# Latent attention by head with a table rope, and modulation by array quarters, in a two-layer diffusion trunk

## The chip, the cores and the metric

The kernel runs on one core of a Trainium2 chip. The metric is the device time of one execution in microseconds; three runs of the kernel before took 1910.07, 1912.01 and 1912.65 us. Engines are named PE (TensorE, with PEld for its weight loads), DVE (VectorE), ACT (ScalarE), POOL (GpSimd) and SP (SyncE, which here only issues DMAs).

## The reference

Two layers work on 512 latent tokens and 256 context tokens of 1024 features, all in fp32. A layer computes a modulated RMSNorm, one input projection whose columns feed four mixers, an output projection, and a gated feed-forward block. The second layer makes no context output. What the change touches is the modulation and mixer D, multi-head latent attention (MLA):

```python
def mla_heads(p, q_norm, w_uq, kv_norm, w_ukv, cos, sin, use_rope):
    cq, ckv, k_rot = jnp.split(p, [MLA_Q_RANK, MLA_Q_RANK + MLA_KV_RANK], axis=-1)     # 192, 128, 32
    q = (rmsnorm(cq, q_norm) @ w_uq).reshape(b_sz, t_len, MLA_HEADS, MLA_NOPE + MLA_ROPE)   # 4 x (64 + 32)
    kv = (rmsnorm(ckv, kv_norm) @ w_ukv).reshape(b_sz, t_len, MLA_HEADS, MLA_NOPE + MLA_V_DIM)
    ...
    if use_rope:                                 # latent tokens only
        q_rot = apply_axial_rope(q_rot, cos, sin)
        k_rot = apply_axial_rope(k_rot, cos, sin)    # one rotary key for all four heads
```

Latent queries see all 768 keys, context queries (first layer only) the 256 context keys. The modulation is silu(c) times a matrix of 1024 x 6144 per layer, for the two vectors c and c_ctx; it gives six sections (shift, scale and gate of both halves) of 1024 features.

## The kernel before, in words

Activations stand feature by token: a tile is 128 features (partitions) by 768 tokens. Every product of fp32 operands is made of three matmuls of a rounded type (fp32r): each operand is split in a high part (ACT casts) and a low part (DVE subtracts in `split`, L136 to L138; POOL subtracts in `psplit`, L140 to L142), and high·high, low·high and high·low are summed in PSUM. All matmuls pass the helper `mm`, so they stand at line L134 and are told apart by their tiles. PSUM has two pools: `b2`, two tiles of two banks (scores `pss`, projections over all tokens), and `b1`, four tiles of one bank (all the rest: `psm`, `psq`, `psk`, `psv`, transposed probabilities `pspt`, values `psy`, output projection `pso`). SBUF tiles come from rotating pools `s3` (768 columns) and `w4` (1024 columns).

The program is written as Python generators; `run` interleaves several of them by weights (each `yield` ends a step), and a scheduler then fixes the order of each engine's queue ahead of time, by estimated times. The stage in question is L1248:

```python
        run((chain(scan(), late()), 1.0), (chain(some_mods(NS), mla_prologue(), attention(mla_halves)), WM))
```

The scan (mixer B, six chunks; tiles `pscr`, `pstt`, `psg`, `psyo`, `psyb`) runs beside, first, eight modulation chunks, then the MLA prologue, then the MLA attention. `late` splits the outputs of the mixers A, B and C for the output projection.

*Modulation* (`mod_chunks`, L196). A chunk makes 512 of the 6144 features. The vectors stand as 32 columns (two of them used) of a stationary operand, so a matmul fills 32 columns of the array; the four quarters of the array work on four k tiles at once, and the four partial sums stand in four groups of 32 PSUM rows. ACT copies the 128 x 512 result (`mrow`, L208), four fp32 products with the constant `sel` (two columns) add up the quarters and turn features to partitions, DVE adds the bias.

*MLA prologue* (`mla_prologue`, L1113). Values `vd` for the four heads; a query projection of all four heads' rotary rows (four times 32 rows) with rope by `rope` (L496: DVE shuffle and cosine product, POOL sine product, DVE add, into `qr`); then per pair of heads `get_pair`: query and key projections, and per head operands `dqh`, `dql`, `dkh`, `dkl` with 64 rows of the head, 32 rotary rows copied in from `qr` and `kr` (L1170, L1171, `psplit`), and 32 padded rows by POOL (L1154).

*The rotary key* `kr` is made far earlier, in the input projection, by the same `rope` on 32 rows (`q_then`, L842).

*Attention* (`attention`, L585) has a unit for each head and 128 queries: `scores` (scores in `pss`, row maximum on DVE L524, exponential on ACT L531, scaling on POOL L538), three units later `turn` (transposes `pspt`, split), then `values` (`psy`, L582 and L583). `AHEAD` = 10 units ahead of a unit's scores its operands are prepared. There are 20 units in the first layer and 16 in the second, where only latent tokens ask.

After the stage the output projection reads the split outputs (`pso`, `out_tile` L1258); its stream `x` is loaded by SP just ahead of it.

Of the kernel before, what the change touches and what calls it, by code (L numbers as in the profile page):

```python
# [34 lines left out]
AHEAD = 10  # L35
NA, NC, NS = 0, 0, 12
# [7 lines left out]
NP1 = 8  # L44
# [21 lines left out]
for _n, _w in PARTS:  # L66
# [4 lines left out]
CONSTS = [("ident", 128), ("ones", 128), ("sel", 2), ("fnw", 8), ("cosA", 512), ("sinA", 512), ("cosM", 512),  # L71
          ("sinM", 512), ("uf", 128), ("ub", 128), ("bones", 128)]
# [16 lines left out]
def trunk(ctx: ExitStack, tc: tile.TileContext, a, out):  # L89
# [106 lines left out]
    def mod_chunks(l, chs):  # L196
        for ch in chs:
# [16 lines left out]
            yield  # L214

# [266 lines left out]
    def mixers(l, norm, halfway, mods):  # L482
# [102 lines left out]
        def attention(halves):  # L585
# [5 lines left out]
            for i in range(n + LOOK + 1):  # L591
                for j in range(i, min(n, i + AHEAD + 1)):
# [225 lines left out]
        def norm_split(srcs, n, segs, res):  # L818
# [13 lines left out]
            for t, r, w in srcs:  # L832
                hi, lo = s3("chi", F32R), s3("clo", F32R)
# [8 lines left out]
        def q_then():  # L842
            mqn = tiny("mqn", 2)
            dve.tensor_scalar(mqn, par_at(l, "mqn", 0, 2), DS, None, op0=ALU.mult)
            kr.append(s3("kr"))
            rr = slice(64, 96)
            rope(kr[0], dq[1], C("cosM"), C("sinM"), SWAP8, rr)
            act.copy(kr[0][rr, CT], dq[1][rr, CT])
# [7 lines left out]
        d_items = [in_tile(T_DQ, qsegs, d_post(dq, qsegs, 128)), in_tile(T_DX, both, d_post(dq, both, 96, q_then), 96),  # L856
# [256 lines left out]
        def mla_prologue():  # L1113
            wq = [w4("wq", (2, 512)) for _ in range(2)]
            for i, (r, nm) in enumerate(((128, "wuqa"), (64, "wuqb"))):
                wr = w4("raw", (1024,), F32)
                nc.sync.dma_start(wr[:r, :384], a[nm][l])
                split(wq[0][:r, i, :384], wq[1][:r, i, :384], wr[:r, :384])
# [5 lines left out]
            (ckh, ckl), cqs = ckv[0], d_low  # L1124
            vd = [s3("vd", F32R, (6, 128)) for _ in range(4)]
            for j in range(6):
                ps = b1("psv")
                sl = slice(128 * j, 128 * j + 128)
                for jj, (hh, wi) in enumerate(((ckh, 0), (ckl, 0), (ckh, 1))):
                    mm(ps[:, 0:256], hh[:, sl], wk[:, wi, 256:512], jj == 0, jj == 2)  # L1130
                for hd in range(4):
                    split(vd[hd][:, j, 0:64], vd[hd][:, j, 64:128], ps[:, 64 * hd:64 * hd + 64])
                yield

            def up_q(t):
                ps = acc("psq", qsegs)
                for i, r in ((0, 128), (1, 64)):
                    for jj, (wi, lo) in enumerate(((0, 0), (0, 1), (1, 0))):
                        for s, p in zip(qsegs, ps):
                            mm(p, wq[wi][:r, i, 128 * t:128 * t + 128], cqs[i][lo][:r, SEG[s]], i == 0 and jj == 0,  # L1140
                               i == 1 and jj == 2)
                return ps

            ps = up_q(2)
            qr, qrw = s3("qr"), s3("qrw", F32, (SEQ,))
            act.copy(qrw, ps[0])
            rope(qr, qrw, C("cosM"), C("sinM"), SWAP8)
            if wc:
                act.copy(qr[:, CT], ps[1])
            yield  # L1150
            halves = mla_halves

            def pad_rows(t, w):
                pool.tensor_copy(t[96:128, :w].rearrange("p (a b) -> p a b", b=64),  # L1154
                                 ident[96:128, 0:64].unsqueeze(1).to_broadcast([32, w // 64, 64]))

            for pr in range(2):
                def get_pair(pr=pr):
                    qps = up_q(pr)
                    r = []  # L1160
                    for hh in range(2):
                        hd = 2 * pr + hh
                        rh = slice(64 * hh, 64 * hh + 64)
                        qh_, ql_ = s3("dqh", F32R), s3("dql", F32R)
                        for t in (qh_, ql_):
                            pad_rows(t, QW)
                        for s, p in zip(qsegs, qps):
                            split(qh_[0:64, SEG[s]], ql_[0:64, SEG[s]], p[rh])
                        q4 = qr[32 * hd:32 * hd + 32, :QW]
                        act.copy(qh_[64:96, :QW], q4)  # L1170
                        dve.tensor_tensor(ql_[64:96, :QW], q4, qh_[64:96, :QW].bitcast(F32), op=ALU.subtract)  # L1171
                        r.append([qh_, ql_])
                    kps = acc("psk", both)
                    for jj, (wi, hh) in enumerate(((0, ckh), (0, ckl), (1, ckh))):
                        for s, p in zip(both, kps):
                            mm(p, wk[:, wi, 128 * pr:128 * pr + 128], hh[:, SEG[s]], jj == 0, jj == 2)
                    for hh in range(2):
                        rh = slice(64 * hh, 64 * hh + 64)
                        kh_, kl_ = s3("dkh", F32R), s3("dkl", F32R)
                        for t in (kh_, kl_):  # L1180
                            pad_rows(t, TOK)
                        for s, p in zip(both, kps):
                            split(kh_[0:64, SEG[s]], kl_[0:64, SEG[s]], p[rh])
                        psplit(kh_[64:96], kl_[64:96], kr[0][64:96])
                        r[hh] += [kh_, kl_]
                    y_d.append(s3("yf"))
                    return r, y_d[-1]

                get_pair = once(get_pair)
                for hh in range(2):  # L1190
                    hd = 2 * pr + hh

                    def sc_mm(ps, q0, segs, get_pair=get_pair, hh=hh):
                        qh_, ql_, kh_, kl_ = get_pair()[0][hh]
                        qs = slice(q0, q0 + 128)
                        for jj, (q_, k_) in enumerate(((qh_, kh_), (ql_, kh_), (qh_, kl_))):
                            for o, sl in segs:
                                mm(ps[:, o:o + sl.stop - sl.start], q_[:, qs], k_[:, sl], jj == 0, jj == 2)

                    def yf(get_pair=get_pair):  # L1200
                        return get_pair()[1]

                    def vhl(hd=hd):
                        return vd[hd]

                    def no_sink():
                        return None

                    for hb in range(2):
                        def score(ps, qi, hb=hb, sc_mm=sc_mm):  # L1210
                            sc_mm(ps, 256 * hb + 128 * qi, ((0, LAT), (512, CT)))
                            return TOK, 0
# [381 lines left out]
```

## Time and profile before

| | |
|---|---|
| median of three runs | 1912.01 us (1910.07 to 1912.65) |
| the profiled execution | 1910.93 us, span 1909.1 us |
| PE busy | 1813.2 us (95%), 11552 matmuls |
| DVE / ACT / POOL busy | 1071.2 (56%) / 788.9 (41%) / 537.7 us (28%) |
| mean granted clock of PE | 0.975 |
| stage of layer 0, scan start to first `pso` | 320.65 to 472.42 us |
| first MLA scores, layer 0 / layer 1 | 406.81 / 1423.55 us |
| stage of layer 1 | 1345.61 to 1476.93 us |

The page puts the engines' slices over time, the chain of waits, and groups of instructions side by side. Busy shares are means over stages with different limits, so this stage is cut in windows: modulation with scan, prologue, attention. In the rows below "xN" counts instructions; a fp32 matmul that is not split stands as two. The bracket at a row's end is the time its engine waited ahead of it, and what released it. The granted clock has two levels, 1.2 and 2.4 GHz; PEclk is the mean over a stretch as a share of the upper one.

### The profile page before, as it was taken

How to read it: one execution, taken by the hardware profiler on the slowest of the kernel's cores; microseconds unless marked ns; L12 is line 12 of the kernel's file. 1: busy time of each engine (PE TensorE's matmuls, PEld its weight loads, DVE VectorE, ACT ScalarE, POOL GpSimd, SP SyncE). 2: the span in 40 equal slices, each digit the busy share in tenths (PEclk: the TensorE clock that was granted, in tenths of full speed). 3: DMA queues.
4: the chain of work that ended last, by engine and by line, in shares of the span. 5: the costliest groups of instructions: out<-in, count | busy, mean ns of one | idle time of the engine just before them, and what ended most of it. 6: DMA issues, size and time to landing. Idle time of an engine off the chain costs nothing. (4 is left out here: it accounts for less than half of the span.)

```text
span 1909.1 us, 29269 instructions
## 1 busy us (share of the span) xinstructions
PE 1813.2 (95%) x11552; PEld 1573.8 (82%) x11552; DVE 1071.2 (56%) x2058; ACT 788.9 (41%) x1506; POOL 537.7 (28%) x565
## 2 busy tenths in 40 slices
PE   6989999978999999999999999999988999999997
PEld 3978898757888888888888888989767888888886
DVE  4564674467355444554553474677367565555545
ACT  3475564457243222222222354655447352323222
POOL 0353421544155143122230054440344210000001
PEclk9999899989999999999999999999979999999999
DMA  8101016303212222222221210103703322323221
GB/s 314 42 12 45 24 56 247 119 1 133 78 56 80 87 89 78 78 81 75 88 68 56 95 50 12 56 23 123 288 1 109 100 79 88 111 83 117 78 89 55
DMA packets 50568, 165.19 MB, mean 87 GB/s; under 512 B 5632, under 2 KB 9600, under 8 KB 50304
## 3 DMA queue, kind: packets, MB, share of 16 engines
q1 hardware_dynamic: 50432, 163.33, 25.1%
q8 instruction: 91, 1.49, 0.3%
q14 instruction: 45, 0.37, 0.1%
HBM read 159.12 MB, written 4.19 MB: 86 GB/s over the span
## 5 line engine op out<-in xcount | busy, mean ns | idle before, releaser
L134 PE MATMUL psi<-hhi,whi 128*128 128x256 f32 (+2 forms) x1600 | 492.4, 330 | 4.7 <-DVE fc L1350 2.5
L134 PE MATMUL psi<-hlo,whi 128*128 128x256 f32 (+2 forms) x1600 | 488.7, 328 | 0.0
L134 PE MATMUL psi<-hhi,wlo 128*128 128x256 f32 (+2 forms) x1600 | 488.0, 328 | 0.0
L138 DVE TENSOR_TENSOR wlo<-raw,whi 128x1024 fp32r<-128x1024 f32 (+2 forms) x188 | 239.9, 1276 | 158.6 <-ACT whi L137 116.5
L134 PEld LDWEIGHTS psi<-hhi,whi 128*128 128x128 f32 (+1 forms) x1600 | 288.6, 190 | 32.9 <-DVE fc L1350 2.7
L137 ACT CAST whi<-raw 128x1024 fp32r<-128x1024 f32 (+2 forms) x188 | 195.0, 1039 | 284.3 <-DMA raw<-in_wup_dram 117.3
L134 PEld LDWEIGHTS psi<-hhi,wlo 128*128 128x128 f32 (+1 forms) x1600 | 288.5, 190 | 26.2
L134 PEld LDWEIGHTS psi<-hlo,whi 128*128 128x128 f32 (+1 forms) x1600 | 288.6, 190 | 25.7
L1312 DVE SCALAR_TENSOR_TENSOR x<-psd,mod,x 128x512 f32<-128x512 f32 (+1 forms) x248 | 153.2, 644 | 177.9 <-PE psd L134 176.9
L323 POOL TENSOR_TENSOR sq<-sq,sq 128x256 f32<-128x256 f32 (+1 forms) x45 | 44.9, 998 | 553.6 <-ACT sq L321 532.4
L134 PE MATMUL psd<-ulo,whi 128*128 128x512 f32 (+1 forms) x552 | 167.9, 349 | 0.0
L134 PE MATMUL psd<-uhi,wlo 128*128 128x512 f32 (+1 forms) x552 | 167.3, 348 | 0.0
L134 PE MATMUL psd<-uhi,whi 128*128 128x512 f32 (+1 forms) x552 | 166.2, 348 | 0.0
L538 POOL TENSOR_SCALAR p<-p,sm 128x768 f32<-128x768 f32 (+3 forms) x120 | 100.0, 838 | 173.9 <-DVE sm L536 97.4
L227 POOL TENSOR_SCALAR mtmp<-wm,cact 128x256 f32<-128x256 f32 x112 | 64.8, 594 | 187.9 <-DMA wm<-in_wmod_dram 147.5
L531 ACT ACTIVATE p<-pss,nm 128x768 f32<-128x768 f32 (+3 forms) x120 | 93.0, 777 | 55.3 <-DVE nm L524 21.1
L1331 ACT ACTIVATE fc<-psi,par 128x512 f32<-128x512 f32 (+1 forms) x60 | 42.4, 707 | 175.8 <-PE psi L134 175.7
L524 DVE TENSOR_REDUCE nm<-pss 128x1 f32<-128x768 f32 (+2 forms) x96 | 84.7, 884 | 45.1 <-PE pss L134 44.8
L134 PEld LDWEIGHTS psd<-uhi,whi 128*128 128x128 f32 x552 | 94.4, 189 | 13.5
L134 PEld LDWEIGHTS psd<-uhi,wlo 128*128 128x128 f32 x552 | 93.7, 189 | 14.1
L134 PEld LDWEIGHTS psd<-ulo,whi 128*128 128x128 f32 x552 | 93.3, 189 | 13.5
L560 PE MATMUL pspt<-con,p 128*128 128x128 f32 x528 | 82.9, 277 | 4.4 <-POOL p L538 2.0
(277 smaller groups left out, 3282.7 us busy)
## 6 DMA issues: line engine op xcount, KB each, us to landing
wm<-in_wmod_dram SPq DMA_DIRECT2D x96, 512.0 KB, 6.5
raw<-in_wup_dram SPq DMA_DIRECT2D x88, 512.0 KB, 3.4
raw<-in_wdn_dram SPq DMA_DIRECT2D x44, 512.0 KB, 3.3
raw<-in_win_dram SPq DMA_DIRECT2D x34, 512.0 KB, 3.6
raw<-in_wout_dram SPq DMA_DIRECT2D x16, 512.0 KB, 3.4
x<-in_xT_dram SPq DMA_DIRECT2D x8, 384.0 KB, 6.5
x<-in_xT_dram SPq DMA_DIRECT2D x8, 256.0 KB, 7.5
xd<-x SPq DMA_DIRECT2D x8, 256.0 KB, 2.0
```

The source lines that it names most:

```text
L134: pe.matmul(out, lhsT, rhs, start=start, stop=stop, **kw)
L137: act.copy(hi, src)
L138: dve.tensor_tensor(lo, src, hi.bitcast(F32), op=ALU.subtract)
L227: pool.tensor_scalar(tmp[:, t], wm[:, g], cact[:, 4 * q + g, t:t + 1], 1.0, op0=ALU.mult, op1=ALU.mult)
L323: eng.tensor_tensor(self.sq[0][:, sl], self.sq[0][:, sl], sq[:, sl], op=ALU.add)
L524: dve.tensor_reduce(nm, ps[:, :width], axis=AX.X, op=ALU.max, negate=True)
L531: act.activation(p[:, i], v[:, i], AF.Exp, bias=nm[:, i:i + 1], accum_out=sm[:, i:i + 1])
L538: pool.tensor_scalar(p[:, i], p[:, i], sm[:, i:i + 1], 1.0, op0=ALU.mult, op1=ALU.mult)
L560: pe.transpose(pt[:, 128 * (j - j0):128 * (j - j0) + 128], p[:, 0, 128 * (j - t0):128 * (j - t0) + 128], ident)
L1312: dve.scalar_tensor_tensor(x[m][:, sl], p, mod[l][:, s, 40 + m:41 + m], x[m][:, sl], op0=ALU.mult, op1=ALU.add)
L1331: act.activation(c[:, b:e], p, AF.Identity, bias=par_at(l, "fcb", j), scale=par_at(l, "fcw", 3 * j + 1))
```

## The change

The changed `mod_cols` takes one section of 1024 features. Each quarter of the array works on another 256 features, all with the same k tile, and the eight k tiles accumulate in PSUM; so nothing has to be added across quarters. Two transposes per section turn the features to partitions. The 32 transfers of 512 KB and the 128 column-tiled matmuls of a layer stay.

```diff
+    def mod_cols(l, s):
+        ps = b1("psm")
+        for k in range(KD):
+            wm = w4("wm", (4, 256), F32)
+            nc.sync.dma_start(wm, a["wmodc"][l, s - 2, k])
+            for g in range(4):
+                mm(ps[32 * g:32 * g + 32, 0:256], cact[:, k, :], wm[:, g, :], k == 0, k == KD - 1, tile_position=(0, 32 * g))
+            if k % 2:
+                yield
+        row = s3("mrow", F32, (256,))
+        act.copy(row, ps[:, 0:256])
+        for i in range(2):
+            pe.transpose(ps[:, 256 + 128 * i:384 + 128 * i], row[:, 128 * i:128 * i + 128], ident)
...
+        for t in range(2):
+            dve.tensor_tensor(dst[:, t], got[:, :, :, t], bias, op=ALU.add)
+        yield
...
-        mods = [(l, ch) for ch in range(4, 12)] if l == 0 else [(l, ch) for ch in range(12 - NP1, 12)]
+        mods = [(l, s) for s in range(2, 6)]
```

The rotary key comes out of the input projection twice, as it is and with swapped halves (the weight's columns are laid out so). One product with the table `ropeT` (cosine rows, sine rows) and one fp32 matmul with the constant `dup`, which adds the two, replace the shuffle and its products. It stands in 64 rows, the 32 rotary rows twice:

```diff
-            rope(kr[0], dq[1], C("cosM"), C("sinM"), SWAP8, rr)
-            act.copy(kr[0][rr, CT], dq[1][rr, CT])
+            kt = s3("kt")
+            dve.tensor_tensor(kt, dq[1], C("ropeT"), op=ALU.mult)
+            ps = acc2("pskr", both)
+            for s, p in zip(both, ps):
+                mm(p, C("dup"), kt[:, SEG[s]], True, True)
+            for s, p in zip(both, ps):
+                act.copy(kr[0][64:128, SEG[s]], p[64:128])
```

In the MLA prologue a head's query projection gives all 128 rows: 64 plain, 32 rotary, 32 rotary with swapped halves. A table product makes them ready to split; the scores' own sum over rows adds the two rotary halves. Low and high part of the 64-row query input stand in one tile, so five matmuls per head do what six did per group. `get_pair` becomes `get_head`; the keys' PSUM tiles (`get_k`) serve two heads. `AHEAD_D` = 6 for this attention:

```diff
-            for pr in range(2):
-                def get_pair(pr=pr):
...
+            def get_k(pr):
+                if pr not in kps:
+                    kps[pr] = acc("psk", both)
...
+            for hd in range(4):
+                def get_head(hd=hd):
+                    qh_, ql_, t = s3("dqh", F32R), s3("dql", F32R), s3("dqt")
+                    ps = acc("psq", qsegs)
+                    hs = slice(128 * hd, 128 * hd + 128)
+                    for jj, (w, hh) in enumerate(((wq[0][:, 0, hs], cqh), (wq[0][:, 0, hs], cql), (wq[1][:, 0, hs], cqh),
+                                                  (wq[0][:, 1, hs], cqs), (wq[1][:, 1, hs], cqs))):
                         for s, p in zip(qsegs, ps):
...
+                            mm(p, w, hh[:, SEG[s]], jj == 0, jj == 4)
+                    for s, p in zip(qsegs, ps):
+                        dve.tensor_tensor(t[:, SEG[s]], p, C("ropeT")[:, SEG[s]], op=ALU.mult)
+                    split(qh_[:, :QW], ql_[:, :QW], t[:, :QW])
+                    rh = slice(64 * (hd % 2), 64 * (hd % 2) + 64)
+                    kh_, kl_ = s3("dkh", F32R), s3("dkl", F32R)
+                    for s, p in zip(both, get_k(hd // 2)):
+                        split(kh_[0:64, SEG[s]], kl_[0:64, SEG[s]], p[rh])
+                    if k0:
+                        for dst, src in zip((kh_, kl_), k0):
+                            pool.tensor_copy(dst[64:128], src[64:128])
+                    else:
+                        split(kh_[64:128], kl_[64:128], kr[0][64:128])
+                        k0[:] = [kh_, kl_]
+                    return qh_, ql_, kh_, kl_
...
-        run((chain(scan(), late()), 1.0), (chain(some_mods(NS), mla_prologue(), attention(mla_halves)), WM))
+        run((chain(scan(), late()), 1.0), (chain(some_mods(NS), mla_prologue(), attention(mla_halves, AHEAD_D)), WM))
```

The scheduler orders the queues anew. PE in layer 0, where the modulation (`psm`) runs beside the scan; before:

```order
L134 MATMUL psm<-wm,cact 32x256 x16
L134 MATMUL psm<-con,mrow 128x2 x4
L134 MATMUL pstt<-xw,btk 128x128 x8
L134 MATMUL psm<-con,mrow 128x2 x4
L1022 MATMUL pscr<-con,z 128x128 x8
```

And of the change, at the same place of the scan (L229 are the transposes):

```order
L134 MATMUL psm<-wm,cact 32x256 x2
L134 MATMUL pstt<-xw,btk 128x128 x4
L134 MATMUL psm<-wm,cact 32x256 x16
L134 MATMUL pstt<-xw,btk 128x128 x4
L1051 MATMUL pscr<-con,z 128x128 x4
L229 MATMUL psm<-con,mrow 128x128 x2
L1051 MATMUL pscr<-con,z 128x128 x4
L134 MATMUL pstt<-xw,btk 128x128 x2
L134 MATMUL psm<-wm,cact 32x256 x15
```

The products with `sel` are gone. Over the stage the column-tiled matmuls stood in 15 runs in each layer; now they stand in 17 in layer 0 and 22 in layer 1. The modulation ends with two of six scan chunks done; before it was four.

DVE in layer 0, the last rows up to the first row maximum of the MLA attention (`nm<-pss`); before:

```order
L138 TENSOR_TENSOR dql<-psq,dqh 64x512
L138 TENSOR_TENSOR dql<-psq,dqh 64x256
L138 TENSOR_TENSOR dkl<-psk,dkh 64x512
L138 TENSOR_TENSOR dkl<-psk,dkh 64x256
L138 TENSOR_TENSOR dkl<-psk,dkh 64x512
L138 TENSOR_TENSOR dkl<-psk,dkh 64x256
L501 TENSOR_TENSOR qr<-qr,rsh 128x512
L1171 TENSOR_TENSOR dql<-qr,dqh 32x768 x4
L524 TENSOR_REDUCE nm<-pss 128x1
```

Of the change (L1189 is the table product, `yb` and `z` belong to the scan):

```order
L138 TENSOR_TENSOR dkl<-psk,dkh 64x512
L1189 TENSOR_TENSOR dqt<-psq,con 128x512
L138 TENSOR_TENSOR dkl<-psk,dkh 64x256
L1189 TENSOR_TENSOR dqt<-psq,con 128x256
L138 TENSOR_TENSOR dkl<-kr,dkh 64x768
L138 TENSOR_TENSOR dql<-dqt,dqh 128x768
L138 TENSOR_TENSOR dkl<-psk,dkh 64x512
L1091 SCALAR_TENSOR_TENSOR yb_3876<-xbc_2691,par_69,psyb 128x128
L1091 SCALAR_TENSOR_TENSOR yb_3877<-xbc_2883,par_69,psyb 128x128
L138 TENSOR_TENSOR dkl<-psk,dkh 64x256
L1065 TENSOR_TENSOR z<-z,psg 128x256 x2
L545 TENSOR_REDUCE nm<-pss 128x1 x2
```

Before, the operands of all four heads stood ahead of the first row maximum; now those of two heads do, with scan work between, and the heads 2 and 3 are prepared among the attention's units. The low parts of `y_a`, `y_b` and `y_c` (POOL) move to the attention's end. From the output projection on the order is as before.

## Rows read from the trace of the kernel before

**Rows 1.** The page, busy time of each engine, share of the span, instructions.
```profile
PE 1813.2 (95%) x11552; PEld 1573.8 (82%) x11552; DVE 1071.2 (56%) x2058; ACT 788.9 (41%) x1506; POOL 537.7 (28%) x565
```

**Rows 2.** Windows, layer 0: length, busy us (instructions) by engine, PEclk, DMA share, GB/s.
```profile
230.00:320.00 90.00, 89.24 (x744) 86.71 (x743) 59.73 (x151) 47.89 (x110) 16.71 (x18) 1.00 0.33 112
320.65:372.26 51.61, 51.02 (x533) 37.13 (x531) 19.12 (x46) 26.79 (x82) 24.87 (x27) 1.00 0.52 195
372.26:406.81 34.55, 28.30 (x154) 20.74 (x152) 21.33 (x58) 19.10 (x53) 23.83 (x22) 0.82 0.00 1
406.81:472.42 65.61, 54.17 (x351) 45.37 (x351) 51.11 (x110) 47.54 (x108) 29.82 (x30) 0.96 0.25 89
```

**Rows 3.** Windows, the same three stretches in layer 1.
```profile
1345.61:1397.87 52.26, 51.39 (x529) 36.69 (x527) 18.88 (x43) 23.52 (x68) 26.65 (x34) 1.00 0.52 194
1397.87:1423.55 25.68, 17.70 (x78) 13.27 (x77) 18.72 (x60) 15.31 (x45) 12.50 (x10) 0.71 0.00 1
1423.55:1476.93 53.38, 46.89 (x289) 39.23 (x289) 40.08 (x77) 38.02 (x82) 22.01 (x22) 0.92 0.27 89
```

**Rows 4.** PE's groups, 320.65 to 372.26: busy us, mean ns of one, idle before.
```profile
L134 PE MATMUL psm<-wm,cact 128*32 128x256 f32 x256 | 18.1, 384 | 0.3 <-DVE hst L1010 0.3
L134 PE MATMUL psm<-con,mrow 128*128 128x2 f32 x64 | 8.2, 250 | 0.3 <-ACT mrow L208 0.3
L1022 PE MATMUL pscr<-con,z 128*128 128x128 f32 x48 | 6.4, 277 | 0.0
L134 PE MATMUL pstt<-xw,btk 128*128 128x128 f32 x40 | 5.8, 287 | 0.0
```

**Rows 5.** PE's groups in layer 1, 1345.61 to 1397.87.
```profile
L134 PE MATMUL psm<-con,mrow 128*128 128x2 f32 x56 | 7.1, 248 | 0.3 <-ACT mrow L208 0.3
```

**Rows 6.** Timeline of PE: start us, length us, instruction.
```profile
328.44 0.63 PE L134 MATMUL psm<-wm,cact 128*32 128x256 f32 x4
...
330.02 1.93 PE L134 MATMUL psm<-wm,cact 128*32 128x256 f32 x32
```

**Rows 7.** Timeline ahead of the first scores of layer 0.
```profile
386.83 1.38 POOL L500 TENSOR_TENSOR rsh<-rsh,con 128x512 f32<-128x512 f32 x1 [1.57 <-DVE rsh L498]
...
405.07 0.68 DVE L501 TENSOR_TENSOR qr<-qr,rsh 128x512 f32<-128x512 f32 x1
...
406.81 1.62 PE L134 MATMUL pss<-dkh,dqh 128*128 128x512 f32 x4 [3.74 <-ACT dqh L1170]
```

**Rows 8.** Timeline, first scores of layer 1.
```profile
1423.55 1.62 PE L134 MATMUL pss<-dkh,dqh 128*128 128x512 f32 x4 [6.79 <-ACT dqh L1170]
```

**Rows 9.** DVE's groups, 372.26 to 472.42: busy us, mean ns of one, idle before.
```profile
L1171 DVE TENSOR_TENSOR dql<-qr,dqh 32x768 fp32r<-32x768 f32 x4 | 3.8, 949 | 1.2 <-ACT dqh L1170 0.9
...
L138 DVE TENSOR_TENSOR dql<-psq,dqh 64x512 fp32r<-64x512 f32 x4 | 2.8, 688 | 4.3 <-ACT dqh L137 4.3
...
L138 DVE TENSOR_TENSOR dql<-psq,dqh 64x256 fp32r<-64x256 f32 x4 | 1.7, 415 | 1.0 <-ACT dqh L137 1.0
```

**Rows 10.** Timeline of PE, score matmuls of 512 and 256 columns at full clock.
```profile
449.84 0.51 PE L134 MATMUL pss<-dkh,dql 128*128 128x512 f32 x2
...
450.19 0.51 PE L134 MATMUL pss<-dkl,dqh 128*128 128x512 f32 x2
```

**Rows 11.** Timeline, a value tile (`psy`) and a transpose tile (`pspt`), written to read.
```profile
464.21 0.36 PE L134 MATMUL psy<-phi,vd 128*128 128x256 f32 x1 [1.92 <-DVE yf L583]
...
464.54 0.63 PE L560 MATMUL pspt<-con,p 128*128 128x128 f32 x4
...
465.82 0.69 DVE L138 TENSOR_TENSOR plo<-pspt,phi 128x512 fp32r<-128x512 f32 x1 [0.50 <-ACT phi L137]
...
467.31 0.42 DVE L583 TENSOR_TENSOR yf<-psy,yt 64x256 f32<-64x256 f32 x1
```

**Rows 12.** Timeline of POOL, the last softmax scaling of the attention.
```profile
462.29 1.70 POOL L538 TENSOR_SCALAR p<-p,sm 128x256 f32<-128x256 f32 x2 [0.53 <-PE pspt L560]
```

**Rows 13.** POOL's groups, 372.26 to 472.42.
```profile
L142 POOL TENSOR_TENSOR ylo<-yf,yhi 128x768 fp32r<-128x768 f32 x4 | 7.3, 1826 | 4.0 <-issue 3.3 <-ACT yhi L141 0.6
```

More of the change, by code (lines that the diff above doesn't have):

```diff
@@ L35 @@
 AHEAD = 10
+AHEAD_D = 6
 NA, NC, NS = 0, 0, 12
@@ L43 @@
 STEP = 256
-NP1 = 8
 WP = 0.3
@@ L583, in values, with attention @@
             dve.tensor_tensor(hf.yf()[64 * hf.hh:64 * hf.hh + 64, hf.tok0:hf.tok0 + 256], yp[0:64, 0:256], t, op=ALU.add)
-        def attention(halves):
+        def attention(halves, ahead=AHEAD):
             units = []
@@ L591, in attention @@
             for i in range(n + LOOK + 1):
-                for j in range(i, min(n, i + AHEAD + 1)):
+                for j in range(i, min(n, i + ahead + 1)):
                     units[j][0].prep()
@@ L1114, in mla_prologue @@
             wq = [w4("wq", (2, 512)) for _ in range(2)]
-            for i, (r, nm) in enumerate(((128, "wuqa"), (64, "wuqb"))):
+            for i, nm in enumerate(("wuqa", "wuqb")):
                 wr = w4("raw", (1024,), F32)
-                nc.sync.dma_start(wr[:r, :384], a[nm][l])
-                split(wq[0][:r, i, :384], wq[1][:r, i, :384], wr[:r, :384])
+                nc.sync.dma_start(wr[:, :512], a[nm][l])
+                split(wq[0][:, i], wq[1][:, i], wr[:, :512])
             wr = w4("raw", (1024,), F32)
@@ L1131, in mla_prologue @@
                 for hd in range(4):
-                    split(vd[hd][:, j, 0:64], vd[hd][:, j, 64:128], ps[:, 64 * hd:64 * hd + 64])
+                    split(vd[hd][:, j:j + 2, 0:64], vd[hd][:, j:j + 2, 64:128], pv[:, :, hd])
                 yield
[L1135 to L1138, printed above, removed]
-                        for s, p in zip(qsegs, ps):
-                            mm(p, wq[wi][:r, i, 128 * t:128 * t + 128], cqs[i][lo][:r, SEG[s]], i == 0 and jj == 0,
-                               i == 1 and jj == 2)
-                return ps
@@ L1144, in mla_prologue @@
[L1144 to L1155, printed above, removed]
@@ L1157, in mla_prologue @@
-            for pr in range(2):
-                def get_pair(pr=pr):
[L1159 to L1212, printed above, removed]
-                        halves.append(Half(get_pair, score, ALL6, vhl, yf, hh, 256 * hb, no_sink, False))
-                    if wc:
-                        def score(ps, qi, sc_mm=sc_mm):
-                            sc_mm(ps, 512 + 128 * qi, ((0, CT),))
-                        halves.append(Half(get_pair, score, CTX2, vhl, yf, hh, SEQ, no_sink, True))
@@ new lines, in mla_prologue @@
+            halves = mla_halves
+            kps = {}
+            def get_k(pr):
+                if pr not in kps:
+                    kps[pr] = acc("psk", both)
+                    for jj, (wi, hh) in enumerate(((0, ckh), (0, ckl), (1, ckh))):
+                        for s, p in zip(both, kps[pr]):
+                            mm(p, wk[:, wi, 128 * pr:128 * pr + 128], hh[:, SEG[s]], jj == 0, jj == 2)
+                    y_d.append(s3("yf"))
+                return kps[pr]
+            k0 = []
@@ L1228, in some_mods @@
             for _ in range(min(n, len(mods))):
-                i, hc = mods.pop(0)
-                yield from mod_chunks(i, [hc])
+                yield from mod_cols(*mods.pop(0))
         run((gqa(aq, ak, vta[0], None, False, y_a), 1.0), (gemm(c_items), 0.3), (some_mods(NA), WA))
@@ L1553, in _layout @@
     putc("sinA", np.tile(sa, (2, 1)))
-    putc("cosM", np.tile(cm, (4, 1)))
-    putc("sinM", np.tile(sm, (4, 1)))
     i = np.arange(128)
     k_, l_ = i[:, None], i[None, :]
+    rt = np.ones((128, TOK), f)
+    rt[64:96, :SEQ], rt[96:, :SEQ], rt[96:, SEQ:] = cm, sm, 0.0
+    putc("ropeT", rt)
+    putc("dup", ((k_ >= 64) & (l_ >= 64) & (k_ % 32 == l_ % 32)).astype(f))
     putc("ident", np.eye(128, dtype=f))
```

62 lines of the change are left out of this document (46 added, 16 removed).

## The prediction, made before the result was known

> **What bounds the kernel now.** The page comes first. TensorE is busy for 95% of the span [rows 1], so a microsecond leaves the end only where TensorE loses work, loses waiting, or gets its full clock back. The edits sit in one stage of each layer: the scan with the modulation beside it, then the MLA prologue, then the MLA attention, up to the first matmul of the output projection. So the second view is that stage cut in three windows, in layer 0 [rows 2] and in layer 1 [rows 3]. The reader is to see three regimes. In the first window (modulation beside the scan) TensorE idles 0.6 us of 51.6 at granted clock 1.00: every matmul taken out there is worth its duration. In the second (MLA prologue) TensorE is busy only 28.3 us of 34.55, and the mean clock is 0.82; in layer 1 it is 17.7 of 25.68 at 0.71. In the third (attention) it idles 11.4 and 6.5 us at clocks 0.96 and 0.92. DMA has nothing to do with the second window: its share there is 0.00.
>
> To make waiting and clock comparable I turn the mean clock into lost time. At level 1.2 GHz work takes twice as long as at 2.4; a mean of 0.82 over 34.55 us is 12.4 us at the low level, of which half, 6.2, is loss. The third window gives 2.6 in the same way; layer 1 gives 7.4 and 4.3. With the idle time (0.6 + 6.25 + 11.44 in layer 0; 0.87 + 7.98 + 6.49 in layer 1), **idle plus clock loss** is 27.1 us in layer 0 and 27.0 in layer 1. This is the whole of what a better order can give back.
>
> The third view is the timeline at the first scores [rows 7, 8]. The low-half rope of the queries (`qr`) had its sine product from POOL at 388.2, but DVE's closing add ran at 405.07, because DVE's queue holds the splits of all four heads ahead of it; the first scores follow at 406.81, after a wait of 3.74 us for the cast of `qr`. In layer 1 TensorE waits 6.79 us there. So what ends last ahead of the attention is the preparation of all heads at once.
>
> **The change part by part.** *Modulation.* The 128 column-tiled products a layer and their 32 transfers stay. The selector products go: 64 instructions, 8.2 us in layer 0 [rows 4]; in layer 1 56 of them in the window make 7.1 [rows 5], and with the eight outside it, at the same 0.127 us, 8.1. Eight transposes come in; a transpose of 128 columns takes 0.133 us (`pscr`, 6.4 us by 48) [rows 4], so +1.1. ACT's and DVE's share of it shrinks too, but neither is late here (27 and 19 us busy of 52 [rows 2]).
>
> The column-tiled products are now interleaved with the scan in smaller runs. The rows show that a run has an entry price: 32 in a row take 1.93 us (0.060 each), four take 0.63 where 0.24 would do [rows 6], so up to 0.39 a run; over all 15 runs it is (18.1 − 256×0.060)/15 = 0.18 [rows 4]. The new order has 17 runs in layer 0 and 22 in layer 1: +0.4 and +1.5, at most +0.8 and +2.7. The Trainium skill ("TensorEngine Tiling (Array Packing)", section "Tiling Modes", its key properties) gives a reason that speaks against this change: TensorE drains when the tiling mode changes. The rows of short runs agree; by it the price is per change of mode and not per matmul, and 9 more runs could not eat the 14 us that the selector products free.
>
> *MLA matmuls.* Queries go up by head, four heads of five products, instead of three groups of six: two more products, of 512+256 columns each in layer 0. Such a pair takes 0.35 us at full clock (449.84 to 450.19) [rows 10], so +0.7; in layer 1, 512 columns, +0.5. These three items make −6.0 in layer 0 (−8.2+1.1+0.4+0.7) and −5.0 in layer 1 (−8.1+1.1+1.5+0.5), in a place with no idle time to swallow them.
>
> *Key rope by a matmul.* Two fp32 products with `dup` over 768 columns come into the input projection, where TensorE is saturated (the stretch from 230 to 320 us: 89.24 of 90 [rows 2]). No fp32 product of that width is in the trace. Six transposes of 128 columns would take 0.8; six fp32 products of 128 columns, at two instructions of 0.145 (`pstt`, 5.8 us by 40 [rows 4]), 1.74. I take 1.5 a layer, nearer to the fp32 row. Nothing is given back for the shuffle and rope on DVE and POOL that go, which lay beside this work.
>
> *Prologue.* Ahead of the first scores the old order has all heads; the new one has values, two heads' queries, and one pair's keys. The path is DVE's queue for head 0: its two table products, the split of 128x768, four key splits, one rope split, two products of head 1. By the nearest rows (512 columns 0.69, 256 columns 0.42, 768 columns 0.95 [rows 9]) this is about 5.5 us, 6.7 with the waits for ACT between. TensorE has 2.8 us of `psk` and `psq` of head 1 beside it (eight pairs of 0.35). So the hole is about 4 us a layer, with scan work put between the first scores. In place of 6.25 idle and 6.2 clock loss (layer 1: 7.98 and 7.4) I put 4 (layer 1: 5, since less scan is left to fill it). That the splits of the heads 2 and 3 now come inside the attention, and so do the scan's last chunks, I cost at nothing: over the stage DVE loses `dql<-qr` (3.8 us [rows 9]) and the rope, POOL loses the padding copies, and in the attention window DVE is busy 51 of 65.6 us. If that cover is gone, rival A tells the price.
>
> *Attention.* Its own idle time and clock loss I leave: 11.4+2.6 in layer 0, 6.5+4.3 in layer 1. Then idle plus clock loss is 18 (27.1 before: −9.1) and 16 (27.0: −11.0). The lower bound on this item is no gain at all; the upper, the prologue's hole filled by the scan and the attention's losses halved, leaves 8 and 6.
>
> *The end of the stage.* The low parts of `y_a`, `y_b`, `y_c` move to the end: five POOL subtractions of 1.83 us, 9.2 in all, behind POOL's last work for the softmax at 462.29 + 1.70, with the output projection starting at 472.42 [rows 2, 12, 13]. 8.4 us of cover and an output projection that starts on other tiles: zero, or at most 2 us a layer. After this stage the order of the instructions is the same.
>
> Sum: layer 0 −6.0 −9.1 +1.5 = −13.6; layer 1 −5.0 −11.0 +1.5 = −14.5; together −28.1. The profiled execution took 1910.93 us (span 1909.1), so 1882.8; the median of the runs is 1.1 above it: **1884**. From bounds: with no order gain −28.1+20.1 = −8.0, so 1904; with the upper bound (8 and 6 in place of 18 and 16) 1864.
>
> **The rivals.** *A: the wait only moves.* The attention now prepares heads one at a time, and each new head has a chain like head 0's. If TensorE waits for heads 1, 2 and 3, and stays at 1.2 GHz through it, idle plus clock loss remains 54 and only the matmuls count: 1904. For it: in the attention the clock is 0.92 to 0.96 even now, and it falls when TensorE has holes (0.71 in the window with 31% idle [rows 3]). The Trainium skill ("TensorE: Matmul & The Clock Gate", section "Part 1: The HAM clock gate") has TensorE drop to the half clock after idling; the trace agrees, 0.82 and 0.71 are both in the windows with the most idle time. Against it: the new heads come due three and more units ahead, with scan matmuls between.
>
> *B: denser than costed.* With scan left over for the prologue and for the attention, the holes fill: 1864. For it: two of six scan chunks are still to run, 64 us of attention has 11.4 us idle to take them. Against: `ACT p` and the value chain that hold `pss` are not touched.
>
> *C: slower, by PSUM.* There are four one-bank buffers. `psk` of heads 2 and 3 takes two of them from head 2's preparation to head 3's (5 units in layer 0, 4 in layer 1), while `psq` and the scan's norm ask for more. A unit of attention holds a transpose buffer for 464.54 to 466.51 = 2.0 us, a half-wide one some 1.2, and half of a value buffer's 3.5 (464.21 to 467.73) [rows 11]: 5.0 buffer-us. With four buffers this allows a unit each 1.25 us, with two 2.5, with one 5.0; the cadence now is 65.61/20 = 3.28. With two left nothing is lost. With one left a unit loses 1.7 us; over the 9 units with `psk` held that is 15 us, over all 36 units 61 us, so 1943. It decides from the point where the mean cadence is above about 4.1 us (28/36 = 0.8 us a unit more), where the result is slower than before.
>
> *D: no change.* The end of the stage is set by something not moved, such as the transfers of `x` and the weights that SP issues for the output projection: 1908 to 1914. Nothing in the windows points there: the DMA share is 0.25.
>
> **How the numbers follow.** Forecast 0.62, with its own range from 1872 to 1894; A 0.17, B 0.10, C 0.07, D 0.04. About 0.2%, 3.8 us, is what a measurement can tell from no change. The forecast, A and B are faster by more, 0.89, less 0.02 for a weak end of A: 0.87. Within are that end and 0.03 of D, 0.05; slower are C and 0.01 of D, 0.08. The range is 1864 to 1904: it leaves out C, D and the far ends of A and B.
>
> **What would show it.** Right: no `psm<-con` of two columns beside the scan and about 18 us of column-tiled products in it; the first `pss` near 377 us in layer 0 in place of 406.8, with a hole of about 4 us ahead, and in layer 1 some 60 us behind the start of its first window in place of 78; the first `pso` about 14 us and 28 us sooner than 472.4 and 1476.9; two `pskr` products of 0.7 to 0.9 us. Wrong: `pss` or `pspt` waiting for `psk` releases or for `dqh` of the heads 1 to 3 for more than 2 us each (A, C); mean clock below 0.9 from the first scores to `pso` (A); `pso` waiting for `ylo` or `x`.

## The result, and the profile after

The changed kernel took 1889.59 us (median of 4 runs, 1880.93 to 1891.58) against 1911.43 us; the ratio is 0.988, with a 95% interval of 0.986 to 0.9899. It is faster by about 22 us where 28 were forecast, inside the stated range. Run again it took 1886.02 us (1883.58 to 1891.74), ratio 0.9863 (0.9846 to 0.9879). The median of all eight runs is 1887.6, and variants are compared with that. The profiled execution has a span of 1889.8 us; at 1891.58 us it is among the slowest of the eight.

The windows below are the stage of layer 0 (to the first MLA scores, then to the first `pso`), then the same two parts of layer 1. The columns are as in [rows 2]; the fences with windows below have them too.

```profile
324.23:382.77 58.54, 54.39 (x521) 37.44 (x519) 24.74 (x64) 29.57 (x96) 26.32 (x28) 1.00 0.45 176
382.77:464.54 81.77, 70.11 (x461) 60.48 (x461) 62.24 (x131) 50.94 (x114) 34.84 (x36) 0.92 0.20 68
1343.07:1399.27 56.20, 53.90 (x531) 36.57 (x529) 27.11 (x65) 27.31 (x84) 20.58 (x23) 1.00 0.48 185
1399.27:1456.03 56.76, 46.84 (x311) 39.80 (x311) 47.97 (x100) 39.45 (x87) 27.22 (x27) 1.00 0.24 84
```

The stage fell from 151.8 to 140.3 us in layer 0 and from 131.3 to 113.0 in layer 1. The half-clock stretch ahead of the scores is gone in this profile (1.00 in both first parts, 0.82 and 0.71 in the prologues of [rows 2, 3]); in a second profile of the changed kernel layer 0 loses 1.7 us there to the clock. The first scores come at 382.77 (a timeline row starts 0.01 sooner), as this piece of TensorE's timeline shows:

```profile
380.88 0.96 PE L134 MATMUL psq<-chi,wq 128*128 128x512 f32 x4
381.68 0.28 PE L134 MATMUL psq<-clo,wq 128*128 128x256 f32 x1
381.80 0.52 PE L134 MATMUL psq<-chi,wq 128*128 128x256 f32 x3
382.76 0.62 PE L134 MATMUL pss<-dkh,dqh 128*128 128x512 f32 x2 [0.45 <-ACT dkh L137]
383.22 0.51 PE L134 MATMUL pss<-dkh,dql 128*128 128x512 f32 x2
383.57 0.53 PE L134 MATMUL pss<-dkh,dqh 128*128 128x512 f32 x2
```

The wait of 3.74 us in [rows 7] is 0.45 here. The next table splits each part's length in idle time, clock loss and the rest (work at full clock). Idle time is length less busy time from windows like those above; clock loss is half of the time that the trace's clock record gives as at the lower level, so it is finer than the rounded mean in the prediction.

| part, us: length = idle + clock loss + work | before | changed |
|---|---|---|
| layer 0, scan to first scores | 86.2 = 6.8 + 6.1 + 73.2 | 58.5 = 4.2 + 0 + 54.4 |
| layer 0, first scores to `pso` | 65.6 = 11.4 + 2.5 + 51.7 | 81.8 = 11.7 + 6.8 + 63.3 |
| layer 0, `pso` to the feed-forward's first `psd` | 117.4 = 4.4 + 3.4 + 109.6 | 123.5 = 7.1 + 8.5 + 107.9 |
| layer 1, scan to first scores | 77.9 = 8.9 + 7.6 + 61.5 | 56.2 = 2.3 + 0 + 53.9 |
| layer 1, first scores to `pso` | 53.4 = 6.5 + 4.4 + 42.5 | 56.8 = 9.9 + 0 + 46.8 |

So the layers' stages gave 11.5 and 18.3 us, 29.8 in all where the two sums without the key rope said 15.1 + 16.0. The rest went elsewhere. The first `pscs` of the scan stands at 324.23 in place of 320.65: 3.6 us, 3.3 of them lost between 205 and 235 us, where the key rope is. And behind layer 0's stage the way to `psd` is 6.1 us longer. There DVE, in its timeline, holds the second weight part:

```profile
462.38 0.69 DVE L138 TENSOR_TENSOR phl<-pspt,phl 128x512 fp32r<-128x512 f32 x1 [0.48 <-ACT phl L137]
463.11 3.24 DVE L138 TENSOR_TENSOR ylo<-yf,yhi 128x768 fp32r<-128x768 f32 x1
466.38 0.42 DVE L604 TENSOR_TENSOR yf<-psy,yt 64x256 f32<-64x256 f32 x1
466.83 1.23 DVE L138 TENSOR_TENSOR wlo<-raw,whi 128x1024 fp32r<-128x1024 f32 x1
```

POOL and TensorE beside it:

```profile
461.87 3.67 POOL L142 TENSOR_TENSOR ylo<-yf,yhi 128x768 fp32r<-128x768 f32 x2
...
468.12 0.80 PE L134 MATMUL pso<-yhi,wlo 128*128 128x512 f32 x1 [2.62 <-DVE wlo L138]
```

The subtraction that takes 0.95 to 0.98 us elsewhere takes 3.24, and ends 0.8 us after POOL's two subtractions (465.54). The one that reads PSUM (`phl`, from 462.38) took its usual 0.69 beside POOL. TensorE waits 2.62 us for `wlo`, and runs its next matmuls at a spacing of 0.43 us until 473, where 0.23 is the spacing of 512 columns at full clock.

### The profile page after: what moved, and what is told of

It reads as the page before. It is cut to its first block, busy times and chain, and to the rows that moved or that the text cites. A ratio compares the mean times of both kernels' runs of the same rounds, so it can differ in the third digit from the quotient of the medians.

```text
span 1889.8 us, 28933 instructions
## 1 busy us (share of the span) xinstructions
PE 1795.6 (95%) x11454; PEld 1560.4 (83%) x11454; DVE 1065.5 (56%) x2022; ACT 768.3 (41%) x1455; POOL 503.6 (27%) x533
## 4 chain that ended last, share of the span: by engine, by line
PE 84%; DVE 7%; ACT 4%; POOL 2%; issue 2%; DMA 1%; SPq 0%; POOLq 0%; DVEq 0%; ACTq 0%
PE psi L134 41%; PE psd L134 16%; PE pso L134 6%; PE psf L134 4%; PE pss L134 3%; PE psy L134 3%; PE psm L134 2%; PE pspt L581 2%; PE psv L134 2%; PE psn L134 1%; DVE nm L545 1%; ACT p L552 1%; PE psnr L134 1%; PE psyb L134 1%; DVE wlo L138 1%
## 5 line engine op out<-in xcount | busy, mean ns | idle before, releaser
L134 PE MATMUL psi<-hhi,whi 128*128 128x256 f32 (+1 forms) x1600 | 493.1, 331 | 4.9 <-DVE fc L1361 2.7
L134 PE MATMUL psi<-hlo,whi 128*128 128x256 f32 (+1 forms) x1600 | 489.8, 328 | 0.0
L134 PE MATMUL psi<-hhi,wlo 128*128 128x256 f32 (+1 forms) x1600 | 488.4, 328 | 0.0
L134 PEld LDWEIGHTS psi<-hhi,whi 128*128 128x128 f32 x1600 | 290.2, 191 | 33.3 <-DVE fc L1361 2.9
L134 PEld LDWEIGHTS psi<-hlo,whi 128*128 128x128 f32 x1600 | 290.3, 191 | 26.1
L134 PEld LDWEIGHTS psi<-hhi,wlo 128*128 128x128 f32 x1600 | 289.7, 191 | 26.2
```

Of the source, the lines that this page charges most:

```text
L134: pe.matmul(out, lhsT, rhs, start=start, stop=stop, **kw)
```

## The experiments

Nine variants, and the changed kernel once more. "Stage" is the length from the scan's start to the first `pso`, layer 0 and layer 1 (before 151.8 and 131.3, changed 140.3 and 113.0).

**The modulation alone.** The kernel before, with `mod_cols` in place of `mod_chunks`:

```diff
-                i, hc = mods.pop(0)
-                yield from mod_chunks(i, [hc])
+                yield from mod_cols(*mods.pop(0))
```

> The kernel before with the new modulation alone (sections by array quarters, transposes in place of the selector products); prologue, attention and rotary key as before. Theory 1 (independent terms): only matmuls leave, 7.4 us in layer 0 and 4.2 in layer 1 by the two traces, idle time and clock loss of the prologue stay near 27 us a layer: about 1900 us. Rival (the modulation's 40 steps became 20, so the prologue starts earlier beside the scan, and that alone fills the hole): half or more of the 19 us of idle and clock loss goes too, 1890 us or less, and the first MLA scores of layer 0 come before 385 us.

Measured: 1909.86 us (12 runs), ratio 0.9997 (0.9986 to 1.0007): nothing. Both theories fell. Windows of its profile (1912.06 us, in the slower half of the twelve runs), layer 0's two parts, then layer 1's first:

```profile
318.81:404.63 85.82, 73.25 (x603) 50.39 (x601) 40.82 (x103) 40.59 (x128) 49.39 (x49) 0.91 0.31 118
404.63:477.25 72.62, 59.60 (x374) 51.87 (x375) 52.59 (x110) 49.30 (x110) 28.99 (x30) 0.90 0.23 81
1349.87:1424.63 74.76, 65.56 (x549) 43.55 (x547) 37.38 (x103) 35.95 (x109) 40.64 (x43) 0.90 0.36 135
```

In layer 0 TensorE has 7.8 us less work in the first part (65.5 for 73.2), yet the part is as long as before: 85.82 for 86.16. The first scores are not TensorE's to start; its DVE, then its TensorE:

```profile
402.89 0.68 DVE L521 TENSOR_TENSOR qr<-qr,rsh 128x512 f32<-128x512 f32 x1
...
404.63 1.62 PE L133 MATMUL pss<-dkh,dqh 128*128 128x512 f32 x4 [4.03 <-ACT dqh L1190]
```

The same chain as in [rows 7] ends last; what TensorE saved became idle time (12.6 us for 6.8) and half clock. The attention behind it is even 7 us longer, by clock loss (7.6 for 2.5) and idle time (13.0 for 11.4). Layer 1 is another matter: there 3.4 us of work leave the first part and it is 3.2 us shorter (74.76 for 77.94), with the attention as before (53.45 for 53.38). So the saving was swallowed in layer 0 and kept in layer 1, and over the whole program no gain can be told from the spread of the runs.

**The prologue and the rotary key alone.** The changed kernel with `mod_chunks` again.

> The changed kernel with the old modulation (chunks, selector products): prologue by head, table rope, rotary key by matmul. Theory 1: matmuls +1.2, rotary key +6.4, idle and clock loss -19, end of the stage +3: about 1903 us. Rival (the gain in the prologue came from the shorter modulation stream): no hole is filled, the rotary key stays as a cost, 1915 to 1922 us, slower than before.

Measured: 1906.09 us (10 runs), ratio 0.9977 (0.9967 to 0.9987). Near theory 1 in time, but not in place. Windows of layer 0 (the profile, 1902.5 us, is of the fastest run, 3.6 us under the median, so its rows show more gain than the median has):

```profile
319.95:387.22 67.27, 65.79 (x636) 49.09 (x634) 30.53 (x75) 33.20 (x100) 26.28 (x28) 1.00 0.41 153
387.22:471.65 84.43, 67.23 (x401) 57.68 (x401) 60.40 (x123) 51.28 (x116) 34.43 (x36) 0.88 0.20 70
```

The scores start 19 us sooner, and the attention is 19 us longer: its idle time is 17.2 us (before 11.4), its clock loss 10.4 (2.5), and 5.1 us of work moved into it. The stage has 151.7 us as before. Layer 1's has 121.8, a gain of 9.5. So alone the parts bring 0 and 4 us, together 22: they don't add.

**Scan work among the units.** In the kernel with the old modulation and in the kernel before, the trace has no scan matmul behind layer 0's first scores, but for the scan's norm (`psn`) in the first of the two; in the changed kernel 60 of the scan's 270 matmul instructions stand there, and the norm. `WM` sets it:

```diff
-WA, WC, WM, WD = 0.3, 0.3, 1.0, 1.0
+WA, WC, WM, WD = 0.3, 0.3, 0.75, 1.0
```

> The changed kernel with weight 0.75 in place of 1.0 for the stream of modulation, prologue and attention, so that in layer 0 all 144 matmul groups of the scan stand ahead of the first MLA scores (before 114, with 30 among the attention's units); layer 1 has none there in either. Theory 1 (scan work among the units fills TensorE's holes there): the first scores come 6 to 8 us later, idle time and clock loss of the attention rise toward the 27 us of the kernel with the old modulation (18.5 in the changed kernel): 1893 to 1896 us. Rival (the units' own chains set the pace, the scan's place is free): 1888 to 1891 us.

Measured: 1901.41 us, ratio 0.9946 (0.9931 to 0.996). The time is beyond theory 1's numbers, and only a part of it lies where theory 1 put it. Windows of layer 0:

```profile
323.36:397.82 74.46, 68.06 (x599) 49.09 (x598) 31.54 (x75) 31.39 (x98) 28.21 (x29) 0.93 0.36 138
397.82:475.23 77.41, 60.71 (x383) 52.00 (x381) 58.01 (x123) 50.28 (x114) 34.82 (x36) 0.93 0.21 76
```

The stage is 151.9 us: layer 0's whole gain is gone, with all the edits in. Idle time among the units is 16.7 us (11.7 with the scan's tail there), although 8 us of work left this part; that is theory 1's mechanism. But clock loss there fell, 5.1 for 6.8, so idle time and clock loss together rose by 3.3 of the 11.6 us. Ahead of the scores they rose by 7.4 (11.5 for 4.2), and counted from the scan's start the first scores come 15.9 us later where 6 to 8 were expected. Layer 1's stage, where no scan work moved past the scores, grew too, to 121.6: there idle time ahead of the scores went from 2.3 to 7.5 us, and 15 of the 20 query matmuls of the heads stand ahead of the scores where 10 did. So the weight does more than place the scan's tail, and layer 0's 11.6 us can't be put down to that place alone. The rest was not tried further.

**Lead of the heads' preparation.** `AHEAD_D` = 10 for 6.

> The changed kernel with the heads prepared 10 units ahead as before, in place of 6: head 2 is prepared right behind head 1, head 3 among the first units. Theory 1 (with 6 the later heads are ready in time, so more lead brings only more splits of DVE ahead of the first row maxima): 1889 to 1893 us. Rival (with 6 TensorE waits for the heads 2 and 3, or their key tiles are held too long in PSUM): 1885 us or less.

Measured: 1883.85 us (1881.47 to 1885.79), ratio 0.9855 (0.9837 to 0.9872): 3.8 us under the changed kernel's eight runs, which themselves lie 10.8 us apart. The rival was nearer in time. In the changed kernel `psy` waits twice for `plo`, with the splits of a new head right ahead of it on DVE; this is DVE, then ACT, then PE, at head 3:

```profile
423.25 0.42 DVE L1189 TENSOR_TENSOR dqt<-psq,con 128x256 f32<-128x256 f32 x1 [0.37 <-PE psq L134]
424.58 0.96 DVE L138 TENSOR_TENSOR dql<-dqt,dqh 128x768 fp32r<-128x768 f32 x1 [0.90 <-ACT dqh L137]
425.45 0.68 DVE L138 TENSOR_TENSOR plo<-pspt,phi 128x512 fp32r<-128x512 f32 x1
```

```profile
423.71 0.83 ACT L137 CAST dqh<-dqt 128x768 fp32r<-128x768 f32 x1 [3.84 <-DVE dqt L1189]
424.45 0.58 ACT L137 CAST phi<-pspt 128x512 fp32r<-128x512 f32 x1
```

```profile
426.19 0.58 PE L134 MATMUL psy<-phi,vd 128*128 128x256 f32 x1 [1.66 <-DVE plo L138]
```

DVE is not short of time (62.2 us of 81.8), and the new head holds `plo` for little: `plo` needs `phi`, which ACT casts until 425.03, so the head's split (`dql`) delays it by 0.4 us of the 1.66, and by as much at head 2. With a lead of 10 the second part of layer 0's stage is 77.4 us in place of 81.8 (idle 10.0 for 11.7, clock loss 1.7 for 6.8, work 65.7 for 63.3); in layer 1 the second part is 3.0 us longer (59.8 for 56.8, most of it clock loss). So what the lead returns in layer 0 is mostly clock, and the rival's waits are not shown as its cause. Head 2 is then prepared right behind the first units' scores, while scan matmuls are still to come.

**The rotary key, placed later.** Table product, matmul and copies behind `norm_split`.

> The changed kernel with the rotary key's table product, matmul and copies moved behind the norm of the query latents, in the program; nothing else changes. Theory 1: of the 3.2 us a layer that the key rope costs, 1.2 is its two matmuls and 2 is the norm's squares on ACT waiting behind the copies out of PSUM; the squares then come first again, about 4 us in all are given back: 1885 to 1886 us. Rival (the 3.2 us are the matmuls and a spell of half clock that falls there anyway): 1889 to 1890 us.

Measured: 1887.52 us, ratio 0.9877 (0.9862 to 0.9892): no gain. In the changed kernel ACT's squares for the norm do stand behind the copies, as its timeline shows (before they began at 208.74):

```profile
213.48 0.85 ACT L876 COPY kr<-pskr 64x512 f32<-64x512 f32 x2 [2.01 <-PE pskr L134]
214.35 1.58 ACT L844 ACTIVATE sq<-dlow 128x768 f32<-128x768 f32 x2
```

In this kernel they begin at 208.62 again, and still the scan starts at 326.49, later than in the changed one. TensorE's idle time up to there is 32.5 us for 30.1. So the order of the squares was not the price, or not alone. TensorE waits for ACT here too: a score matmul 0.4 us for the copies (at 234.51), and the next norm's `psn` 1.7 us for its squares (at 236.93). Neither wait stands in the changed kernel.

**The rotary key without TensorE.** The sum of the two halves by copy and add, also behind the norm:

```diff
-            for s, p in zip(both, ps):
-                mm(p, C("dup"), kt[:, SEG[s]], True, True)
-            for s, p in zip(both, ps):
-                act.copy(kr[0][64:128, SEG[s]], p[64:128])
...
+            act.copy(ku[64:96], kt[96:128])
+            dve.tensor_tensor(kr[0][64:96], kt[64:96], ku[64:96], op=ALU.add)
+            act.copy(kr[0][96:128], kr[0][64:96])
```

> The changed kernel with the rotary key made without TensorE: the table product stays, its sine half is copied to the cosine half's rows (ACT), added (DVE) and the sum copied to the second 32 rows (ACT), all behind the norm of the query latents; no matmul with dup, no PSUM tile for it. Theory 1 (the 3.2 us a layer of the key rope are 1.2 us of matmuls and the rest its two-bank PSUM tile, one of the two that the scores of the attention beside it need): both go, 3 us a layer, about 1883 to 1884 us. Rival (only the matmuls' own time counts, the rest is where spells of half clock fall): 1887 us.

Measured: 1880.91 us (1878.28 to 1883.19), ratio 0.9839 (0.9821 to 0.9858), 6.7 under the changed kernel. The scan of layer 0 starts at 319.68 us, 4.5 sooner. Theory 1 held in size, but its reason is not shown. These are windows between the same two matmuls on either side of layer 0's rope, in the kernel before, the changed one, and this one:

```profile
202.41:236.62 34.21, 34.21 (x265) 33.05 (x265) 20.91 (x57) 16.77 (x37) 10.18 (x8) 0.93 0.10 32
202.74:240.21 37.47, 37.05 (x269) 35.22 (x268) 22.66 (x54) 17.34 (x38) 9.02 (x7) 0.90 0.09 29
200.67:235.65 34.98, 34.57 (x264) 33.15 (x264) 22.37 (x55) 18.61 (x39) 9.90 (x8) 0.94 0.10 31
```

The changed kernel's 3.3 us there are 1.4 of work, 1.5 of clock loss and 0.4 of idle time; TensorE waits for no tile. Without the matmuls 0.8 us are left, and in layer 1 1.5 of 3.0: 4.0 us in all. The rest of this profile's gain lies elsewhere, above all in the way from `pso` to `psd` (115.1 us for 123.5 and 120.2), where no edit is. So the two-bank tile as the part beyond the matmuls is not shown, and the rival's reason (the matmuls, and where the clock falls) fits these rows better.

**The splits of A and C sooner.** `y_a` and `y_c` in a stream of their own.

```diff
...
+            (chain(waits(4), y_split(y_a, 0), y_split(y_c, 4)), 0.15))
```

> The changed kernel with the splits of the outputs of mixers A and C in a stream of their own beside the attention, so that POOL has two low parts behind the last softmax scaling of layer 0 in place of five. Theory 1: DVE's low part of the first MLA output (3.24 us where 0.95 is usual, while POOL subtracts) is held by POOL, and delays the first weight split of the output projection; with POOL free it takes about 1 us, the wait of 2.6 us and the half clock behind it go: 1885 to 1887 us. Rival (DVE is slow there for another reason, or POOL's subtractions inside the attention now hold DVE there instead): 1889 us or more.

Measured: 1883.23 us (1882.56 to 1884.91), ratio 0.9859 (0.9846 to 0.9872). The wait of 2.62 us is gone; DVE's subtraction now stands at 455.92, takes 2.32 us, and again ends 0.8 us after POOL's, early enough for `wlo`. The way from `pso` to `psd` is 116.4 us (123.5 and 120.2 in the two profiles of the changed kernel). The run with the rotary key without TensorE shows the same pair the other way round; first its DVE, then its POOL:

```profile
456.54 1.02 DVE L138 TENSOR_TENSOR ylo<-yf,yhi 128x768 fp32r<-128x768 f32 x1 [0.31 <-ACT yhi L137]
```

```profile
456.69 4.32 POOL L142 TENSOR_TENSOR ylo<-yf,yhi 128x768 fp32r<-128x768 f32 x2
```

There DVE was first by 0.15 us and took 1.02; POOL's two took 4.32 for 3.67. In these traces, who comes first holds the other.

**Combinations.** Both of the last two, and the rotary key without TensorE with a lead of 10.

> Both changes at once: splits of the outputs of A and C in a stream of their own, and the rotary key without TensorE. Theory 1 (independent places): the sum of both gains against 1889.6, 1883.2 less 3 to 6: 1877 to 1880 us. Rival (the gains overlap, or were spells of half clock): 1882 to 1884 us.

> The changed kernel with the rotary key made without TensorE and with heads prepared 10 units ahead in place of 6. Theory 1 (independent places: 3 us a layer in the input projection, and denser units in layer 0): 1875 to 1878 us. Rival (the two gains against 1889.6 are the same chance of clock spells): 1880 to 1884 us.

Measured: 1882.56 us (1880.67 to 1883.7) and 1873.49 us (1873.09 to 1873.93), ratio 0.9802 (0.9787 to 0.9816). The first does not add up: without `pskr` DVE already comes first at the end of the stage, so there was nothing for the earlier splits to mend. The second is the fastest here, 14 us under the changed kernel, more than the 10.5 of both gains together, and 37 under the one before. Its layer 0:

```profile
318.60:379.57 60.97, 56.37 (x521) 39.21 (x519) 25.58 (x64) 29.73 (x96) 26.76 (x28) 0.97 0.44 169
379.57:457.98 78.41, 67.54 (x461) 57.39 (x461) 61.47 (x133) 51.23 (x115) 35.52 (x36) 0.98 0.21 71
```

**The changed kernel again.**

> The changed kernel itself once more, since its four runs went from 1880.9 to 1891.6 us and the variants are compared with their median of 1889.6. Theory 1 (the spread is in which spells fall to half clock, the median holds): 1887 to 1891 us, and the stall ahead of the second weight part of the output projection is in this profile too. Rival (three of the four runs were high by chance): 1882 to 1885 us, and then the rotary key without TensorE, the earlier splits and the longer lead gain little or nothing of their own.

Measured: 1886.02 us, between the two. The stall ahead of `wlo` is in this profile too (way to `psd` 120.2 us), and so is the price of the key rope (scan at 323.83).

## Why the prediction was right, and where it was not

*Matmul work:* right in sum. By the table the work of the stage fell by 7.3 us in layer 0 (forecast 6.0) and 3.3 in layer 1 (5.0). The column-tiled products went from 18.1 to 19.4 us in layer 0 (forecast +0.4) and from 18.5 to 18.4 in layer 1 (forecast +1.5, where seven runs at 0.18 make 1.3), with 17 and 22 runs for 15. The rule of the Trainium skill ("TensorEngine Tiling (Array Packing)", section "Tiling Modes", its key properties) that a change of mode drains TensorE priced nothing that these rows show in layer 1.

*"In a place with no idle time to swallow them":* this step failed as a reason in layer 0. It was read off the first window alone, where TensorE idles 0.6 us. But what stands behind that window, the chain to the first scores, did not start from TensorE's end: with the modulation alone the 7.8 us were swallowed whole. In layer 1 3.2 of 3.4 us were kept. The sum took the parts as independent; in time they gave 0 and 4 us apart and 22 together.

*Prologue:* right in that the hole closes. Idle time and clock loss up to the first scores were put at 4 and 5 us; they are 4.2 and 2.3 (before 12.9 and 16.4). That layer 0's 4 came out is luck: it was to be one hole behind DVE's chain for head 0 (added up too short, by its own rows 6.3 us for 5.5), but ahead of the first scores TensorE waits 0.45 us, and 3.2 of the 4.2 us are scan matmuls (`pscr`) that wait for POOL's `z`.

*Attention:* forecast unchanged at 14 and 10.8 us, measured 18.5 and 9.9. That the sum of both layers came out near is in part luck: preparation by head inside the attention costs (27.6 us of idle time and clock loss with the old modulation in layer 0, for 13.9 before), and the scan's tail among the units fills some of it. Rival A, "the wait only moves", is what layer 0 does in two kernels where no scan is left there (stages of 151.7 and 151.9 us), though in the second more of the added loss stands ahead of the scores than among the units. I gave it 0.17 against the scan matmuls between; they fit what happened, but how much they decide was not separated. That the splits of the heads 2 and 3 inside the attention cost nothing was not borne out (layer 0 idles and loses 18.5 us for 14); the longer lead returned 3.8 us, mostly clock. The prediction also found the half clock in the windows with the most idle time; in layer 0 that holds by share alone, and barely: the attention idles 11.4 us, 17%, at 0.96, the prologue 18% at 0.82.

*Key rope:* the term was mis-sized, 1.5 us a layer for 3.3 in layer 0. In the same way layer 1's is 3.1 (before its key rope the same matmuls ran 5.6 us sooner than before the change, behind it 2.5). The two matmuls take 1.2 us, as bounded, and TensorE idles 0.4 and 0.2 us more; the rest is a longer stretch at half clock, 1.5 and 1.7 us of loss. In layer 1 that part need not be the rope's: with the same rope the kernels with weight 0.75 and with a lead of 10 lose nothing there and pay 1.5 us, and the modulation alone, with the old rope, loses 1.7.

*End of the stage:* put at zero, at most 2 us. POOL's 9.2 us were weighed against the cover until the output projection, as if only `ylo` were waited for. The price came by another way: POOL held DVE, and DVE's `wlo` was late, 2.6 us and part of the clock loss of 8.5 us behind it.

*The signs named ahead:* the first `pso` came 7.9 and 20.9 us sooner, for 14 and 28. No `pss` or `pspt` waits 2 us for a later head, and the clock from the first scores to `pso` is 0.92 and 1.00, so A's signs are absent.

*C* did not occur: with layer 0's units TensorE waits for the key splits once, 0.4 us ahead of the first scores, and the longer lead, which asks for more PSUM at once, was faster.

Not settled: where spells of half clock fall. Between `psd` of layer 0 and the scan of layer 1 the kernel before lost 5.1 us to them and the changed one 3.4, with no edit but the key rope in that stretch, and eight runs of one kernel lie 10.8 us apart. A few us of every comparison here hang on it, and least so that of the last combination, whose four runs lie 0.8 us apart.

## What to carry to other kernels

Work taken off the busiest engine can be swallowed where another engine starts the next stage: follow the chain to the next stage's first instruction before counting a saving, and try the halves of a change apart, since here they brought 0, 4, and together 22 us. Independent matmuls among small dependent steps (attention units with softmax) can fill some of their idle time, here 5 us of it; a stream that ends sooner may be worth more for what it leaves to overlap than for its own time. A gain of a few us between two such kernels should be looked up in the stretch that was edited: of the 6.7 us that the rotary key without TensorE brought, about 4 lay there.

## What the runs showed of the hardware

A DVE subtraction with both operands in SBUF was held while POOL subtracted (3.24, 2.73 and 2.46 us for 0.95, in the changed kernel, in the one with the key placed later and in the one with a lead of 10), each time ending 0.8 us after POOL; POOL took longer when DVE was 0.15 us ahead (4.32 for 3.67). The Trainium skill ("SBUF — State Buffer", section "SBUF: two separate sides") says just this: a DVE operation with two SBUF inputs and a GpSimd one that reads SBUF share a port pair as an exclusive lock, whoever is first keeps it for the whole instruction. The traces agree. In the changed kernel DVE began 0.6 us before the first of POOL's two subtractions ended (463.11, 463.75) and was held through the second too. A DVE operation that reads PSUM was not held (0.69 us beside POOL, its usual time).
